# A decoder layer on one core: pacing of the routing pieces, batched one-hot comparisons and rearranged norms

## The chip, the cores and the metric

The kernel runs on one core of a Trainium2 chip. The metric is device time in microseconds (us), the median over executions. PE is the matmul engine, DVE the vector engine, ACT the scalar engine, POOL the GpSimd engine, SP the engine that mostly issues transfers. A change of under 0.3% (9.5 us here) can't be told from no change.

## The reference, cut to what matters

One layer over 512 tokens of width 2048, in fp32, batch 1, depth 1:

```python
n1 = rms_norm(h, norm1_gain)
q_lat, kv_lat, k_pe, q_swa, k_swa, v_swa = split(n1 @ w_in)         # 2048 x 2112
o_mla = mla_group(...)   # 8 heads, causal, latent q and kv, rotary key part
o_swa = swa_group(...)   # 16 heads, window 128, sinks, relative bias
h = h + concat(rms_norm(o_mla), rms_norm(o_swa)) @ w_out             # 2048 x 2048
xt = rms_norm(h, norm2_gain)
# PEER: 8 heads, two halves of 128 sub-keys each, 16384 experts
q = xt @ w_q;  s = einsum(q, sub_keys)                               # (512, 8, 2, 128)
s_half, i_half = top_k(s, 16)                                        # of 128
top_s, pos = top_k(all 256 sums of the two halves, 16)               # -> expert idx, g = softmax(top_s)
a = xt . expert_u[idx];  w = g * gelu(a)
h = h + sum over the 128 picked experts of w * expert_v[idx]
```

## The kernel before, in words

**Split matmuls.** An fp32 product is made of three matmuls. `split` (L115) writes the high part `hi` on ACT (L117) and the low part `lo` on DVE (L118), and PE multiplies hi·hi, hi·lo and lo·hi (L191 to L193; L897 to L899 in the expert stage). No weight reaches PE before DVE has written its `lo`; that instruction is kept in `mark[0]`. Weights arrive as raw tiles of 1 MB (two `wraw` and one `uraw`), and there are four pairs of part tiles.

**Stages.** In order of time, by the trace: the norm of x with its transposes (to 38 us), the w_in product (to 235), attention (to 470), output norms and w_out product (to 663), the second norm with its transposes (to 705), the w_q product (here `w_pq`, 709 to 883), the U stage (890 to 2074), the V stage (2074 to 3162).

**First norm (L239 to L251).** For each of four blocks of 128 tokens ACT squares and sums, POOL makes the factor `rs` of the root (`rsq`), DVE multiplies `xt` by `rs` and the gain in one instruction (L250), and PE transposes the product (L216).

**Second norm (L709 to L724).** DVE sums `squares` (L712), POOL makes `rs`, DVE writes `n2` in four quarters (L716) and PE transposes it. `n2` has one buffer, so block 1's quarters wait for block 0's transposes. For block 0 DVE also writes `xn0` (L721), the normed rows in their own layout, read by the gathered dot products only.

**U stage.** All 16384 experts are run densely for the last three token blocks (384 tokens), in 128 blocks of 128 experts. `u_block` (L889) has two halves of 24 matmuls. In each half `u_turn` (L876) traces the DVE transpose `uT` (L884) and the split of the half three ahead. The first 128 tokens are done otherwise: `gathered` (L971) fetches 128 rows of U and 128 batches of rows of V by indirect transfers of 1 MB on POOL's queue, with a dot product (L988) or a multiply-add (L991) on DVE for each: 256 gathered tiles in all.

**Fillers.** A `Filler` (L120) holds generators, and `run(budget)` takes pieces from them until their stated costs use the budget up. While it is `paced`, each piece is traced under `issue_after(mark[0])`: on DVE it stands behind the low part traced last. Otherwise the scheduler puts a piece by its priority and its estimate of when operands are ready. Routing (`route`, L756: top 16 by MAX8, FIND_INDEX8 and MATCH_REPLACE, then index arithmetic, all DVE) runs as such pieces, 3.6 per pair of weights in the w_q product and 2.8 per half block in the first U blocks (L1007), not paced. When all 16 routes are done, `dense_gates` (L913) starts as a filler: for each of 384 tokens it builds one-hot matrices of 128 by 128 (`oj` on POOL L921, `on` on DVE L923, `oi` on ACT L926), PE multiplies them into `gps` (L935), and ACT and DVE merge that into `stage` (L944, L945). Each full `stage` is stored to `gates_d` on ACT's queue (L947), 24 times. ACT's queue issues a part of each U load too (L872). The paced filler `gatherer` runs at 1.2 per half block in the U stage (L1035) and at 1.3 per step of 18 matmuls in the V stage (L1082), of which there are 256.

**V stage.** The dense weights `wg` (activations by gates, POOL L1055) are split and multiplied with V (L1065 to L1082), while the gathered tiles that are left run beside it.

## Time and profile before

| | |
|---|---|
| time, median of 3 runs | 3172.58 us (3164.42 to 3173.77) |
| profiled execution: its own time | 3167.54 us |
| its span | 3165.8 us |
| mean granted PE clock | 0.986 |
| PE busy | 3062.2 us, 97% |
| DVE busy | 2411.5 us, 76% |
| ACT, POOL busy | 1273.2 us, 1261.4 us |

A span is from the first to the last instruction; the time adds 1.7 us around it. Busy time is the sum of an engine's instruction times. The share is a mean over all stages; which engine is late in a stage is seen in the windows, which give the busy time of each engine in a stretch of the span, and in the list of PE's waits, which names the instruction that ended a wait.

### The profile page before, as it was taken

The page shows a single profiled execution, that of the slowest core. Times are in us where ns is not written, and L with a number is a line of the kernel's source. Part 1 is how long each engine was busy: PE and PEld are TensorE (multiplying, and loading weights), DVE is VectorE, ACT ScalarE, POOL GpSimd, SP SyncE. Part 2 cuts the span into 40 slices and gives each one's busy share as a digit, 9 for nine tenths or more (in the row PEclk, how much of TensorE's full clock was granted, in tenths as well). Part 3 has the DMA queues.
Part 4 walks back from the last instruction along what each step waited for, and adds up shares of the span by engine and source line. Part 5 has one row for each costly group of instructions (what it writes and reads, how often), then busy time and mean ns, then how long its engine had stood idle before and what let it go on. Part 6 is the DMA issues. An engine that isn't in the chain of part 4 may idle for free.

```text
span 3165.8 us, 43039 instructions
## 1 busy us (share of the span) xinstructions
PE 3062.2 (97%) x15418; PEld 2680.1 (85%) x15418; DVE 2411.5 (76%) x3774; ACT 1273.2 (40%) x2438; POOL 1261.4 (40%) x1324
## 2 busy tenths in 40 slices
PE   8999999989988998999999999999999999999999
PEld 6977767868778998999999998977888888888887
DVE  5425654246997897988999997878888878888784
ACT  5434443232234564655555553323333233232231
POOL 0115320001333765755556663244443334444430
PEclk9998999999999999999999999999999999999999
DMA  5422222244346899899899999989888878888873
GB/s 172 122 80 75 70 97 89 98 120 94 72 97 184 256 288 273 276 277 293 279 289 289 283 309 289 320 322 352 306 306 321 320 284 307 312 314 311 318 264 120
DMA packets 307064, 731.68 MB, mean 231 GB/s; under 512 B 24098, under 2 KB 106274, under 8 KB 269730
## 3 DMA queue, kind: packets, MB, share of 16 engines
q1 hardware_dynamic: 175394, 343.01, 34.6%
q0 software_dynamic: 45056, 293.63, 25.5%
q10 hardware_dynamic: 86400, 92.29, 10.6%
q8 instruction: 122, 2.00, 0.3%
q14 instruction: 92, 0.75, 0.1%
HBM read 666.97 MB, written 61.87 MB: 230 GB/s over the span
## 4 chain that ended last, share of the span: by engine, by line
PE 59%; DVE 12%; DMA 3%; issue 2%; ACTq 1%; ACT 1%; POOL 1%; SPq 0%; DVEq 0%; POOLq 0%
PE pa L899 8%; PE pa L897 8%; PE pa L898 8%; PE acc L191 8%; PE acc L193 8%; PE acc L192 8%; PE tp L191 4%; PE tp L193 3%; PE tp L192 3%; DVE wlo L118 2%; DVE uT L884 2%; DVE gt L988 2%; PE gps L935 1%; DMA wg<-acts_d 1%; ACTq L872 1%
## 5 line engine op out<-in xcount | busy, mean ns | idle before, releaser
L899 PE MATMUL pa<-xTd,wlo 128*128 128x384 f32 x1536 | 521.9, 340 | 12.7 <-DVE wlo L118 12.7
L118 DVE TENSOR_TENSOR wlo<-wraw,whi 128x1024 fp32r<-128x1024 f32 (+3 forms) x229 | 299.4, 1314 | 306.8 <-ACT whi L117 306.6
L897 PE MATMUL pa<-xTd,whi 128*128 128x384 f32 x1536 | 522.7, 340 | 4.1 <-ACT whi L117 4.0
L898 PE MATMUL pa<-xTd,whi 128*128 128x384 f32 x1536 | 521.1, 339 | 0.0
L921 POOL TENSOR_SCALAR oj<-iot,slT 128x128 fp32r<-128x128 f32 x384 | 391.7, 1028 | 295.6 <-PE gps L935 292.6
L117 ACT ACTIVATE whi<-wraw 128x1024 fp32r<-128x1024 f32 (+3 forms) x229 | 232.7, 1022 | 491.0 <-PE acc L193 251.1
L1055 POOL TENSOR_TENSOR wg<-wg,gg 128x384 f32<-128x384 f32 x128 | 231.6, 1828 | 265.3 <-DMA wg<-acts_d 229.9
L991 DVE SCALAR_TENSOR_TENSOR h<-gt,w,h 128x2048 f32<-128x2048 f32 x128 | 319.1, 2493 | 9.8 <-DMA gt<-in_peer_v_dram,eidx 9.8
L980 POOL DMA_INDIRECT gt<-in_peer_v_dram,eidx x128 | 197.1, 1540 | 302.0 <-DVE h L991 282.5
L191 PE MATMUL acc<-whi,wh 128*128 128x512 f32 x768 | 307.8, 401 | 5.5 <-ACT wh L117 5.5
L899 PEld LDWEIGHTS pa<-xTd,wlo 128*128 128x128 f32 x1536 | 292.7, 191 | 14.8 <-DVE wlo L118 14.8
L192 PE MATMUL acc<-wlo,wh 128*128 128x512 f32 x768 | 302.9, 394 | 2.1 <-DVE wlo L118 2.1
L193 PE MATMUL acc<-whi,wl 128*128 128x512 f32 x768 | 304.1, 396 | 0.2 <-DVE wl L118 0.2
L897 PEld LDWEIGHTS pa<-xTd,whi 128*128 128x128 f32 x1536 | 292.9, 191 | 5.7 <-ACT whi L117 5.4
L926 ACT ACTIVATE oi<-on,gT 128x128 fp32r<-128x128 bf16 x768 | 252.2, 390 | 108.8 <-issue 55.8
L988 DVE CUSTOM_DVE_ANT_0 gt<-gt,xn 128x2048 f32<-128x2048 f32 x128 | 293.2, 2291 | 2.9 <-DMA gt<-in_peer_u_dram,eidx 2.9
L898 PEld LDWEIGHTS pa<-xTd,whi 128*128 128x128 f32 x1536 | 292.6, 191 | 0.0
L118 DVE TENSOR_TENSOR wlo<-uT,whi 128x1024 fp32r<-128x1024 f32 x192 | 234.7, 1225 | 43.2 <-ACT whi L117 43.0
L117 ACT ACTIVATE whi<-uT 128x1024 fp32r<-128x1024 f32 x192 | 201.0, 1053 | 160.6 <-DVE uT L884 71.8
L191 PE MATMUL acc<-whi,xT 128*128 128x512 f32 (+2 forms) x624 | 239.7, 384 | 4.6 <-ACT xT L117 2.3
L192 PE MATMUL acc<-wlo,xT 128*128 128x512 f32 (+2 forms) x624 | 234.5, 376 | 4.2 <-DVE wlo L118 4.2
L193 PE MATMUL acc<-whi,xT 128*128 128x512 f32 (+2 forms) x624 | 235.4, 377 | 0.0
(305 smaller groups left out, 6710.8 us busy)
## 6 DMA issues: line engine op xcount, KB each, us to landing
wraw<-in_peer_v_dram SPq DMA_DIRECT2D x86, 1024.0 KB, 5.8
wraw<-in_peer_u_dram ACTq DMA_DIRECT2D x172, 256.0 KB, 7.5
wraw<-in_peer_u_dram SPq DMA_DIRECT2D x172, 256.0 KB, 6.2
uraw<-in_peer_v_dram SPq DMA_DIRECT2D x42, 1024.0 KB, 7.4
acts_d<-ga POOLq DMA_DIRECT2D x128, 192.0 KB, 6.9
gates_d<-stage ACTq DMA_DIRECT2D x24, 1024.0 KB, 13.9
gg<-gates_d SPq DMA_DIRECT2D x16, 1536.0 KB, 7.2
wg<-acts_d SPq DMA_DIRECT2D x128, 192.0 KB, 6.2
```

The source lines that it names most:

```text
L117: first[0] = nc.scalar.activation(hi, src, AF.Copy)
L118: mark[0] = nc.vector.tensor_tensor(lo, src, hi.bitcast(F32), op=ALU.subtract)
L191: nc.tensor.matmul(o, lhs(0, kk, t), w[0][:, k, :n], start=kk == 0, stop=False)
L192: nc.tensor.matmul(o, lhs(0, kk, t), w[1][:, k, :n], start=False, stop=False)
L193: nc.tensor.matmul(o, lhs(1, kk, t), w[0][:, k, :n], start=False, stop=kk == kc - 1)
L897: nc.tensor.matmul(pa[:, :TD], hi[:, k, :], xTd[0][:, kk, :], start=kk == 0, stop=False)
L898: nc.tensor.matmul(pa[:, :TD], hi[:, k, :], xTd[1][:, kk, :], start=False, stop=False)
L899: nc.tensor.matmul(pa[:, :TD], lo[:, k, :], xTd[0][:, kk, :], start=False, stop=kk == KC - 1)
L921: nc.gpsimd.tensor_scalar(oj, iot, slT[1][:, t:t + 1], None, op0=ALU.is_equal)
L926: nc.scalar.activation(oi[:, r, :], on, AF.Copy, scale=gT[r][:, t:t + 1].bitcast(F32))
L988: nc.vector.tensor_tensor_reduce(out=gt, in0=gt, in1=xn0, scale=1.0, scalar=0.0, op0=ALU.mult, op1=ALU.add, accum_out=a[:, s:s + 1])
L991: nc.vector.scalar_tensor_tensor(h[0], gt, w[:, s:s + 1], h[0], op0=ALU.mult, op1=ALU.add)
```

## The change

There are six edits. (1) The first norm's factor `rs` leaves L250: DVE multiplies by the gain alone, the factor is kept in a tile for each block, and the ACT copies that take the w_in product out of PSUM multiply by it. (2) `n2` gets three buffers, and `xn0` is traced after all four blocks of the second norm, behind the low part traced last. (3) The filler is paced from the w_q product until routing has ended. (4) Routing blocks take 1.4 per half instead of 2.8. (5) `on` is made for four tokens by one TENSOR_TENSOR of 128 by 512, 96 in all, with `slT[0]` in bf16. (6) The gatherer's budgets become 1.05 in the U stage and 1.5 in the V stage.

```diff
-        rs = rsq(ss, 1, D)
-        nc.vector.scalar_tensor_tensor(xt, xt, rs, g1, op0=ALU.mult, op1=ALU.mult)
+        rs1.append(rsq(ss, 1, D, name=f"rs1_{t}"))
+        nc.vector.tensor_tensor(xt, xt, g1, op=ALU.mult)
...
-        nc.scalar.activation(n, ps, AF.Copy)
+        nc.scalar.activation(n, ps, AF.Copy, scale=rs1[t])
...
-        n2 = p5n.tile([128, D], F32, name="n2")
+        n2 = p5n.tile([128, D], F32, name="n2", bufs=3)
...
-            nc.vector.scalar_tensor_tensor(xn0, h[0], rs, g2, op0=ALU.mult, op1=ALU.mult)
+            rs_first = rs
...
+    with tc.issue_after(mark[0].ins):
+        nc.vector.scalar_tensor_tensor(xn0, h[0], rs_first, g2, op0=ALU.mult, op1=ALU.mult)
...
+    filler.paced = True
     for c in range(4):
         gemm(stationary, KC, w_pq, c * 512, 512, ev_pq(c), budget=3.6, by_row=True, turn=c)
...
-        slT = [gb.tile([128, TD], F32, name=f"slT{r}") for r in range(2)]
+        slT = [gb.tile([128, TD], BF16 if r == 0 else F32, name=f"slT{r}") for r in range(2)]
...
-            on = gb.tile([128, NK], BF16, name="on", bufs=4)
-            nc.vector.tensor_scalar(on, iotb, slT[0][:, t:t + 1], None, op0=ALU.is_equal)
+            if t % 4 == 0:
+                ons[0] = gb.tile([128, 4, NK], BF16, name="on", bufs=2)
+                nc.vector.tensor_tensor(ons[0], iotb[:, None, :].to_broadcast([128, 4, NK]),
+                                        slT[0][:, t:t + 4, None].to_broadcast([128, 4, NK]), op=ALU.is_equal)
+            on = ons[0][:, t % 4, :]
...
-        u_block(e, 2.8)
+        u_block(e, 1.4)
...
+    filler.paced = False
     filler.add(dense_gates())
...
-        u_block(e, share, 1.2)
+        u_block(e, share, 1.05)
...
-                gatherer.run(1.3)
+                gatherer.run(1.5)
```

What the built program does with it, counted from both programs: routing ends with block 12 of the U stage before and with block 23 now; the dense gates lie over blocks 12 to 113 before and 23 to 117 now; of the 256 gathered tiles 122 are done in the U stage before and 96 now, so 134 and 160 are left to the V stage, where the last stands at step 237 of 256 before and 244 now. The counts of PE, ACT, POOL and SP instructions are the same; DVE has 288 fewer.

**DVE, the first U blocks.** `ulo` and `wlo` are low parts (L118), `uT` the transposes; MAX, MAX_INDEX, MATCH_REPLACE and what works on `ab`, `abf` and `oh` are routing. Before, these rows end a run of 24 routing rows that stands between one `uT` and the next low part:

```order
L786 TENSOR_TENSOR ab<-ab 128x32
L752 MATCH_REPLACE sc<-sv,sc 128x128
L787 CAST abf<-ab 128x32
L751 MAX_INDEX si<-sv,sc 128x8
L788 TENSOR_TENSOR ab<-ab 128x32
L793 TENSOR_TENSOR oh<-abf,iot 128x512
L789 TENSOR_TENSOR abf<-ab 128x32
L753 MAX sv<-sc 128x8
L793 TENSOR_TENSOR oh<-abf,iot 128x512
L118 TENSOR_TENSOR ulo<-uT,uhi 128x1024
L118 TENSOR_TENSOR wlo<-uT,whi 128x1024
L884 STREAM_TRANSPOSE uT<-uraw 128x4x8x32
```

In the change, at the same place of the stage (its lines are numbered three higher in `route`, four higher in `u_turn`):

```order
L118 TENSOR_TENSOR wlo<-uT,whi 128x1024
L753 MAX tv<-cand 128x8
L888 STREAM_TRANSPOSE uT<-uraw 128x4x8x32
L754 MAX_INDEX ti<-tv,cand 128x8
L888 STREAM_TRANSPOSE uT<-wraw 128x4x8x32
L755 MATCH_REPLACE cand<-tv,cand 128x65
L756 MAX tv<-cand 128x8
L757 MAX_INDEX ti<-tv,cand 128x8
L118 TENSOR_TENSOR wlo<-uT,whi 128x1024
L753 MAX tv<-cand 128x8
L118 TENSOR_TENSOR wlo<-uT,whi 128x1024
L754 MAX_INDEX ti<-tv,cand 128x8
```

The long run of routing rows between two low parts is now cut into runs of one to seven rows, each behind a low part.

**DVE, the second norm.** `ss` are the sums, `n_...` the quarters of `n2`, `xn_5857` is `xn0`, `h_...` the last merges of the w_out product. Before:

```order
L712 TENSOR_REDUCE ss<-squares 128x1
L721 SCALAR_TENSOR_TENSOR xn_5857<-h_4852,rs,g_4856 128x2048
L689 TENSOR_TENSOR h_4854<-acc,h_4854 128x512
L689 TENSOR_TENSOR h_4855<-acc,h_4855 128x512
L716 SCALAR_TENSOR_TENSOR n_5873<-h_4852,rs,g_4856 128x16x32 x2
L118 TENSOR_TENSOR wlo<-wraw,whi 128x1024
L716 SCALAR_TENSOR_TENSOR n_5873<-h_4852,rs,g_4856 128x16x32 x2
L712 TENSOR_REDUCE ss<-squares 128x1 x3
L118 TENSOR_TENSOR xT_5869<-tp,xT_5868 128x512 x4
```

In the change:

```order
L713 TENSOR_REDUCE ss<-squares 128x1
L690 TENSOR_TENSOR h_4854<-acc,h_4854 128x512
L713 TENSOR_REDUCE ss<-squares 128x1
L690 TENSOR_TENSOR h_4855<-acc,h_4855 128x512
L717 SCALAR_TENSOR_TENSOR n_5873<-h_4852,rs,g_4856 128x16x32 x4
L717 SCALAR_TENSOR_TENSOR n_5911<-h_4853,rs,g_4856 128x16x32
L118 TENSOR_TENSOR wlo<-wraw,whi 128x1024
L118 TENSOR_TENSOR xT_5869<-tp,xT_5868 128x512 x4
L717 SCALAR_TENSOR_TENSOR n_5911<-h_4853,rs,g_4856 128x16x32 x3
```

`xn_5857` has left its place behind the first sum, the second sum stands before the last merge, and a quarter of the second block stands ahead of the first transposed parts. `xn_5857` now stands behind the last transposed parts of the stage:

```order
L118 TENSOR_TENSOR xTd_5864<-tp,xTd_5863 128x4x128 x4
L717 SCALAR_TENSOR_TENSOR n_5989<-h_4855,rs,g_4856 128x16x32
L118 TENSOR_TENSOR xTd_5864<-tp,xTd_5863 128x4x128 x4
L727 SCALAR_TENSOR_TENSOR xn_5857<-h_4852,rs,g_4856 128x2048
L118 TENSOR_TENSOR ulo<-wraw,uhi 128x1024 x2
L118 TENSOR_TENSOR wlo<-uraw,whi 128x1024 x2
```

**ACT, the dense gates.** `gates_d<-stage` is the store of a full stage, `uraw` and `wraw` from `in_peer_u_dram` are the U loads on this queue. Before, around the first store:

```order
L944 ACTIVATE stage<-gps 128x2x16x8
L904 ACTIVATE ga<-pa 128x384
L117 ACTIVATE whi<-uT 128x1024
L947 DMA gates_d<-stage 128x16x128
L872 DMA uraw<-in_peer_u_dram 32x4x512 x2
L926 ACTIVATE oi<-on,gT_9174 128x128
```

In the change, the first store:

```order
L117 ACTIVATE uhi<-uT 128x1024
L117 ACTIVATE whi<-uT 128x1024
L954 DMA gates_d<-stage 128x16x128
L908 ACTIVATE ga<-pa 128x384
L951 ACTIVATE stage<-gps 128x2x16x8
L933 ACTIVATE oi<-on,gT_9933 128x128
L933 ACTIVATE oi<-on,gT_9934 128x128
L933 ACTIVATE oi<-on,gT_9933 128x128
L933 ACTIVATE oi<-on,gT_9934 128x128
L876 DMA wraw<-in_peer_u_dram 32x4x512 x2
```

Before, a U load follows the store directly; now six rows stand between the store and the next load.

## Rows read from the trace of the kernel before

**Rows 1.** The page, busy time, share of the span and instructions of each engine.

```profile
PE 3062.2 (97%) x15418; PEld 2680.1 (85%) x15418; DVE 2411.5 (76%) x3774; ACT 1273.2 (40%) x2438; POOL 1261.4 (40%) x1324
```

**Rows 2.** Waits of PE: us in total, times, the longest.

```profile
PE pa L899 <- DVE wlo L118: 12.7, 7, 7.6
PE gps L935 <- DVE stage L945: 12.7, 3, 10.3
PE tp L216 <- DVE xt L250: 11.1, 1, 11.1
PE tp L958 <- DVE ij L805: 8.9, 3, 4.1
PE tp L216 <- DVE ss L712: 6.8, 1, 6.8
```

**Rows 3.** Windows: length, busy (count) PE PEld DVE ACT POOL, PEclk, DMA share, GB/s.

```profile
650.00:700.00 50.00, 42.35 (x205) 34.22 (x205) 30.99 (x45) 15.60 (x28) 2.88 (x8) 0.93 0.47 132
800.00:850.00 50.00, 48.64 (x233) 39.62 (x231) 47.38 (x239) 13.27 (x19) 19.33 (x32) 1.00 0.34 78
850.00:900.00 50.00, 40.51 (x183) 33.10 (x184) 47.38 (x213) 10.62 (x15) 15.17 (x28) 0.93 0.40 90
900.00:950.00 50.00, 44.83 (x264) 43.72 (x263) 50.00 (x208) 22.67 (x28) 18.98 (x30) 0.97 0.42 97
950.00:1000.00 50.00, 41.59 (x209) 39.53 (x209) 41.83 (x124) 20.32 (x35) 21.72 (x27) 0.90 0.59 169
890.00:1000.00 110.00, 88.81 (x481) 85.16 (x480) 101.83 (x376) 44.35 (x66) 45.97 (x62) 0.92 0.48 125
1250.00:1300.00 50.00, 39.69 (x221) 39.31 (x220) 37.54 (x54) 24.11 (x59) 26.91 (x25) 0.90 0.86 265
2100.00:2150.00 50.00, 47.89 (x205) 37.94 (x204) 48.27 (x45) 15.65 (x20) 24.89 (x14) 1.00 0.94 362
```

**Rows 4.** Windows of line L897 alone (16 per block): length, PE, PEld, clock, DMA.

```profile
890.40:993.50 103.10, 45.71 (x129) 25.76 (x128) 0.92 0.46 120
993.50:1096.60 103.10, 63.87 (x191) 35.75 (x190) 1.00 0.82 232
```

**Rows 5.** Timeline of DVE, 884 to 900: start, us, instruction.

```profile
886.41 0.24 DVE L753 MAX8 sv<-sc 128x8 f32<-128x128 f32 x1
...
897.28 2.40 DVE L118 TENSOR_TENSOR wlo<-uT,whi 128x1024 fp32r<-128x1024 f32 x2
```

**Rows 6.** Groups of DVE instructions, 890 to 1000: busy us, mean ns.

```profile
L118 DVE TENSOR_TENSOR wlo<-uT,whi 128x1024 fp32r<-128x1024 f32 x15 | 17.9, 1223 | 0.0
L884 DVE STREAM_TRANSPOSE uT<-wraw 128x1024 f32<-128x1024 f32 x13 | 15.5, 1214 | 0.0
L793 DVE TENSOR_TENSOR oh<-abf,iot 128x512 f32<-128x512 f32 x12 | 11.2, 932 | 0.0
```

**Rows 7.** Timeline of DVE, 663 to 674.

```profile
662.85 2.35 DVE L721 SCALAR_TENSOR_TENSOR xn<-h,rs,g 128x2048 f32<-128x2048 f32 x1 [0.94 <-POOL rs L113]
...
672.07 0.69 DVE L118 TENSOR_TENSOR xT<-tp,xT 128x512 fp32r<-128x512 f32 x1 [1.71 <-ACT xT L117]
```

**Rows 8.** Timeline of DVE, 0 to 24.

```profile
8.71 2.35 DVE L250 SCALAR_TENSOR_TENSOR xt<-xt,rs,g 128x2048 f32<-128x2048 f32 x1 [5.08 <-POOL rs L113]
```

**Rows 9.** Line L923, DVE: ns min/median/max, first and last start.

```profile
L923 DVE TENSOR_SCALAR on<-iotb,slT x384: 201/247/607, 993.7 to 1924.0; 128x128 bf16<-128x128 bf16 x192
```

**Rows 10.** Timeline of ACT, 1245 to 1270.

```profile
1246.62 0.39 ACTq L947 DMA_DIRECT2D gates_d<-stage  x1
...
1252.70 10.96 ACTq L872 DMA_DIRECT2D uraw<-in_peer_u_dram  x2
1263.70 0.69 ACT L926 ACTIVATE oi<-on,gT 128x128 fp32r<-128x128 bf16 x2 [15.18 <-issue]
```

**Rows 11.** Windows: the long middle of the expert stages.

```profile
1050.00:2050.00 1000.00, 977.25 (x5680) 973.13 (x5679) 894.12 (x1223) 536.94 (x1246) 586.08 (x595) 0.99 0.96 289
2150.00:3100.00 950.00, 949.87 (x4071) 764.06 (x4070) 786.05 (x636) 290.13 (x337) 389.10 (x233) 1.00 0.83 307
```

More of the change, by code (lines that the diff above doesn't have):

```diff
@@ L105, in gain_rows, with rsq @@
         return t
-    def rsq(ss, n, width, post=1.0):
-        r = small.tile([128, n], F32, name="rs", tag=f"rs{n}")
+    def rsq(ss, n, width, post=1.0, name=None):
+        r = small.tile([128, n], F32, name=name, bufs=1) if name else small.tile([128, n], F32, name="rs", tag=f"rs{n}")
         with tc.high_priority(offset=150):
@@ L238, in block_kernel @@
     p0 = pool("p0", bufs=2, stack=st0)
+    rs1 = []
     for t in range(NT):
@@ L323, in ev_kv @@
         w = KVR + ROPE
-        nc.scalar.activation(n[:, :w], ps[:, :w], AF.Copy)
+        nc.scalar.activation(n[:, :w], ps[:, :w], AF.Copy, scale=rs1[t])
         nc.scalar.activation(sq[:, :KVR], n[:, :KVR], AF.Square, accum_out=ss)
@@ L340, in ev_ks @@
         n = p1w.tile([128, QR], F32, name="latn", bufs=4)
-        nc.scalar.activation(n[:, :2 * HD], ps[:, :2 * HD], AF.Copy)
-        nc.scalar.activation(vsw[:, t, :], ps[:, 2 * HD:4 * HD], AF.Copy)
+        nc.scalar.activation(n[:, :2 * HD], ps[:, :2 * HD], AF.Copy, scale=rs1[t])
+        nc.scalar.activation(vsw[:, t, :], ps[:, 2 * HD:4 * HD], AF.Copy, scale=rs1[t])
         k3 = n[:, :2 * HD].rearrange("p (g d) -> p g d", g=2)
@@ L359, in f @@
             qn = p1w.tile([128, QR], F32, name="latn", bufs=4)
-            nc.scalar.activation(qn, ps, AF.Copy)
+            nc.scalar.activation(qn, ps, AF.Copy, scale=rs1[t])
             q3 = qn.rearrange("p (h d) -> p h d", h=8)
@@ L913, in dense_gates @@
     def dense_gates():
-        slT = [gb.tile([128, TD], F32, name=f"slT{r}") for r in range(2)]
+        slT = [gb.tile([128, TD], BF16 if r == 0 else F32, name=f"slT{r}") for r in range(2)]
         gT = [gb.tile([128, TD], F32R, name=f"gT{r}") for r in range(2)]
-        hot, banks, stages = {}, {}, {}
+        hot, banks, stages, ons = {}, {}, {}, {}
         LAG = 7
```

## The prediction

> **What bounds the kernel now.** I read the page first, then PE's waits, then the windows of the stages where they fall, and only then the timelines. The page has PE busy for 97% of the span [rows 1], so what can be won is PE's idle time, what a lowered clock costs after it, and nothing else: the matmuls are the same before and after. PE's waits say where [rows 2]: on low parts in the U stage (12.7 us in seven waits, one of 7.6), on the merge of the dense gates (12.7, one of 10.3), on the first norm (11.1), on the index sums of routing (8.9) and on the second norm (6.8). Four of these five name DVE instructions that the change moves. The windows [rows 3] show how they bunch: the four from 800 to 1000 have PE busy for 48.64, 40.51, 44.83 and 41.59 of 50, which is 24.4 us of idle time. The granted clock there is 1.00, 0.93, 0.97 and 0.90, a mean of stretches at 2.4 GHz and, after idle times, at 1.2; a shortfall of the clock can cost at most 50 us times that shortfall, 10.0 together. DVE is at 47.38, 47.38 and 50.00 of 50 in the first three of them: there DVE is the bound. Beside it, line L897, 16 times per block, is there 129 times in 103.1 us and then 191 times in the same length [rows 4]: eight blocks at 12.9 us against twelve at 8.6. By this the first eight blocks lose 34 us, of which the idle time and the clock explain nearly all.
>
> The reason is a matter of order. From 886.41 to 897.28 DVE runs routing [rows 5] and only then the two low parts for which PE waits 7.6 us. DVE had the work of a later need ahead of that of a nearer one.
>
> **The change, part by part.**
>
> Routing in the first U blocks (paced, 1.4 for 2.8). DVE's work in a block now: from 890 to 1000 it is busy for 101.83 [rows 3]. Low parts are 1.22 us each, transposes 1.21 [rows 6], and a block has two of each: 4.9. In 110 us, at 12.9 each for the most part, are nine blocks or so, 44 us of such work, which leaves 58 us of routing, 6.4 per block at 2.8 per half. At 1.4 it is half, 3.2. DVE then has 4.9 + 3.2 = 8.1 us per block against PE's 8.6: it fits, by 6%. No piece stands ahead of a low part already traced, so a low part is delayed by one run of pieces (up to seven rows of about 0.28 us, some 2 us) instead of 10.9. Routing lasts until block 23 instead of 12, at no cost to PE while DVE fits. What is late next are the transposes of the index sums: they are ordered among PE's matmuls behind DVE's last reduces, and I leave 3 of their 8.9 us; another 1 to 2 go to the start of the stage. Of 34.4 us (24.4 and 10.0) I take 30 as gone. Bounds: 34 at best, and 13 if DVE stays a little too slow for 23 blocks (below). The same pacing in the w_q product orders the same work at the same budget; its loss in [rows 3] is only 1.4 us, counted above.
>
> Second norm. `xn0`, 2.35 us [rows 7], stands ahead of the last merges and quarters for which PE waits 6.8 us; now it stands behind the stage, and with three buffers the next block's first quarter comes earlier. The wait shrinks by 2.35 and by some of the 0.9 us that DVE waits for POOL ahead of it. The window 650 to 700 has a clock of 0.93 [rows 3], worth up to 3.5 us, part of which goes with it. I take 4; bounds 0 (another operand is as late) and 10 (all of it). `xn0` at its new place is read first by the gathered tiles hundreds of microseconds later.
>
> First norm. DVE waits 5.08 us for the factor `rs` in block 0 [rows 8], and PE's first transpose waits behind that. Without the factor DVE waits for the transfer of `xt` and the gain. Bounds 0 and 5.1, and I take the half, 2.5, since weights must land too before the first product. The multiplication returns inside ACT's copies, which exist anyway: nothing added.
>
> Batched comparisons. 384 instructions at 0.247 [rows 9] are 95 us of DVE. The 96 new ones aren't in this trace. Nearest are two-operand instructions of 512 elements: 0.69 for a low part `xT` [rows 7], 0.93 for `oh` [rows 6], the latter with the same broadcast shape. Below lies 0.25, were 512 elements no dearer than 128. The range is 24 to 89 us, I take 0.69: 66 us, 29 less. All of it lies beside PE at full work: from 1050 to 2050 PE is at 977 of 1000 and DVE at 894 [rows 11]. So it is slack, counted at nothing, unless DVE were the later one at the stalls.
>
> Against this edit speaks a rule of the Trainium skill ("VectorE: DVE Perf Modes", section "The perf-mode tier table"): a comparison with one scalar may run at four elements a cycle in bf16, one with two tensors at two at most, and only with 16-bit operands of step 1, which the broadcast hasn't. By its fp32 formula, (N+151)/0.96 ns, 512 elements are an estimated 0.69 us, 66 us in all; at two a cycle it would be about 0.42, 41 us. The old row's minimum of 201 ns [rows 9] agrees with the fast mode and a large fixed part, so batching gains by the fixed part and loses the mode. Either price is hidden, and the sum above is the same by both.
>
> Dense gates. These begin 11 blocks later and are a little denser (94 blocks for 101). The costly event there isn't DVE's. At 1252.70 two U loads on ACT's queue take 10.96 us to issue, six microseconds after the store of a gate stage, ACT stands for 15.18 [rows 10], and the merge that PE waits for comes 10.3 late [rows 2]; the window loses 10.3 idle and up to 5.0 by the clock of 0.90 [rows 3]. PE's idle time from 1050 to 2050 is 22.7 us in all [rows 11], with the clock's 0.01 below full up to 10 more. Each of the 24 stores and the loads are still there. Their distances change at random: at the first store a load stood directly behind it, and now six rows lie between. I take 5 us less; bounds -26 and +18, the latter being one more stall of that size with its clock.
>
> V stage. 26 gathered tiles move there from the U stage, 27 MB and about 2.3 us of DVE each. From 2150 to 3100 PE is busy for 949.87 of 950, DVE for 786 and the transfers run at 307 GB/s [rows 11]. Adding 26 in some 1040 us makes DVE 84 to 88% busy and 333 GB/s. The window 2100 to 2150 reached 362 with DVE at 48.27 of 50 [rows 3], so both fit. The last tile stands at step 244 of 256, so no tail. I take 0; bounds 0 and +89 (below).
>
> Sum: 30 + 4 + 2.5 + 5 = 41.5. The profiled execution took 3167.5, which gives 3126; it lies 5 below the median of 3172.6, from which it would be 3131. I say 3128.
>
> **The rivals.**
>
> DVE stays the bound in the routing blocks. It is 8.1 of 8.6 by my division, and a fifth more routing per block than I assume (3.8) makes it 8.7, with waits on POOL's products inside the pieces still to come. At 9.2 per block, 23 blocks lose 14 us beyond the forecast; with clock, 17: 3145. For it: DVE was at 50.00 of 50 from 900 to 950. Against: halving is a plain division of a measured load.
>
> The stores' stalls vanish. With DVE lighter and loads further from stores, 26 of the 33 us of the dense stage go instead of 5: 3107. For it: the distance at the first store. Against: the two queues still share what made the load slow, and with 24 stores some will meet a load.
>
> The V stage becomes the bound, the slower side. If transfers can't go beyond the stage's 307 GB/s, the 27 MB cost 27/0.307 = 89 us, and the sum is 3128 + 89 = 3217. It decides from 51 us upward (the gain of 41.5 and the 9.5 that can be told), which 346 MB in the stage need below some 317 GB/s. A milder form is that the whole stage goes like the window 2100 to 2150, PE at 47.89 of 50: 1088 us become 1136, and with 3176 it is no change. For it: PE had waits in just that window, where transfers were busiest. Against: those waits are at the stage's beginning, while later windows have PE full at 307.
>
> The change doesn't do what it says: the tie adds waits of its own and routing delays PE in 23 blocks as it did in 12. Then only the norms' 6.5 count, and 3166 is within the bound. Against: the new order shows low parts at the head of each portion.
>
> **How the numbers follow.** The forecast, 3112 to 3141, has 0.60; DVE still the bound, 3141 to 3160, 0.15; the stalls gone, 3095 to 3112, 0.10; the V stage 0.09, of which 0.05 is slower and 0.04 no change; without effect 0.06, mostly no change, 0.01 slower. A measurement tells 0.3%, 9.5 us, from no change, so faster is below 3163: 0.60 + 0.15 + 0.10 = 0.85; no change 0.04 + 0.05 = 0.09; slower 0.06. The range 3100 to 3158 leaves out the last two rivals and the far ends of the others, about 0.19.
>
> **What would show it.** Right: from 890 on, line L897's blocks come every 8.3 to 8.8 us from the first one, PE has no wait for a low part above 2 us there, and the clock stays at 1.00 from 800 to 1000; DVE is near 47 of 50 until about 1100. PE's first wait ends near 8 to 9 us instead of 11.1, the second norm's wait is 3 to 4 us instead of 6.8, `on` takes 0.65 to 0.75 us, and the V stage has PE full at some 333 GB/s. Wrong: blocks of 9 us and more up to 1100, idle time of PE behind gathered transfers or low parts after 2150, or a store's stall of 10 us more than now.

## The result: 3123.8 us, and two misses of opposite sign

The changed kernel takes 3123.77 us (median of 4 runs, 3121.87 to 3131.22) against 3170.64 for the kernel before (4 runs). The ratio is 0.9856, with a 95% interval of 0.9837 to 0.9874: 47 us less by the medians, 1.4% by the ratio. The forecast was 3128, with a range of 3100 to 3158. The profiled execution is the slowest of the four, 3131.2 us with a span of 3129.5, so the traces account for 36 us of the difference.

The windows say where. First the kernel before, in windows that join those of [rows 3] (length; busy time and count of PE, PEld, DVE, ACT, POOL; granted clock; share of the transfer engines; GB/s):

```profile
750.00:1050.00 300.00, 275.57 (x1419) 247.20 (x1418) 274.04 (x1065) 107.82 (x175) 107.30 (x168) 0.97 0.46 113
1050.00:1900.00 850.00, 833.92 (x4870) 831.91 (x4869) 770.91 (x1104) 487.36 (x1168) 534.35 (x549) 0.99 0.95 287
...
2074.00:2150.00 76.00, 68.34 (x275) 53.43 (x276) 60.95 (x56) 24.20 (x35) 36.79 (x23) 0.96 0.90 343
2150.00:3090.00 940.00, 939.87 (x4029) 755.99 (x4028) 779.46 (x628) 286.95 (x334) 389.10 (x233) 1.00 0.83 307
```

The changed kernel, by the same view. It comes to its V stage at 2012, 61 us earlier:

```profile
650.00:700.00 50.00, 45.69 (x227) 37.23 (x226) 30.64 (x45) 16.85 (x30) 2.88 (x8) 0.97 0.46 137
750.00:1050.00 300.00, 299.56 (x1610) 275.61 (x1609) 278.44 (x964) 101.64 (x130) 80.10 (x135) 1.00 0.50 119
1050.00:1900.00 850.00, 850.00 (x4971) 849.63 (x4970) 762.03 (x902) 515.92 (x1254) 496.13 (x575) 1.00 0.93 274
...
2000.00:2050.00 50.00, 44.20 (x196) 36.32 (x195) 36.53 (x35) 17.82 (x26) 20.35 (x15) 0.97 0.81 301
2050.00:2100.00 50.00, 40.75 (x159) 31.79 (x158) 36.49 (x35) 10.90 (x13) 21.97 (x12) 0.90 0.85 319
2100.00:2150.00 50.00, 45.79 (x188) 35.94 (x188) 44.14 (x42) 12.82 (x14) 23.06 (x16) 0.97 0.90 331
2150.00:3090.00 940.00, 933.91 (x3989) 749.58 (x3988) 799.20 (x651) 283.09 (x330) 435.07 (x242) 1.00 0.88 323
```

From 750 to 1050 PE's idle time went from 24.4 us to 0.4, and the clock from 0.97 to 1.00. From 1050 to 1900 it went from 16.1 us to none, and the clock from 0.99 to 1.00. From the V stage's start to 2150 it grew from 7.7 us to 19.3, with a clock down to 0.90, and after that from 0.1 us to 6.1. A ledger that also counts what half clock costs takes each matmul's distance to the next one and the median distance of its shape in the kernel before, and sums by stage what the first has over the second (us lost):

| stage | before | after | difference | forecast |
|---|---|---|---|---|
| first norm to w_out product (0 to 650) | 84.7 | 84.8 | 0 | -2.5 |
| second norm (650 to 750) | 18.1 | 13.0 | -5 | -4 |
| w_q product and first U blocks (750 to 1050) | 36.5 | 2.2 | -34 | -30 |
| rest of the U stage | 35.8 | 13.9 | -22 | -5 |
| V stage | 18.9 | 44.1 | +25 | 0 |
| sum | 194 | 158 | -36 | -41.5 |

PE's waits in the changed kernel, to be set against [rows 2]:

```profile
PE acc L192 <- DVE wlo L118: 17.6, 10, 6.6
PE tp L216 <- DVE xt L251: 11.2, 1, 11.2
PE acc L192 <- DVE ulo L118: 7.9, 4, 3.5
...
PE tp L216 <- DVE n L717: 3.5, 1, 3.5
...
PE pa L903 <- DVE wlo L118: 0.8, 2, 0.4
```

The low parts of the U stage, 12.7 us before, are down to 0.8 and the gates' merge is gone from the list. On top stand low parts at L192 of `acc`, 25.5 us in 14 waits; all but one wait of 2.2 us, at 22.9 in the w_in product, are in the V stage. The blocks of the U stage come at an even pace, one in 8.3 us, from the third one on (the first two take 12.3 and 10.8); line L901 is what L897 was in [rows 4], and the eight blocks of 12.9 us have become twelve of 8.6:

```profile
887.50:990.60 103.10, 64.39 (x192) 35.85 (x192) 1.00 0.60 145
```

### The profile page after: what moved, and what is told of

The parts are those of the page before. It is cut to its first block, busy times and chain, and to the rows that moved or that the text cites. A ratio compares the mean times of both kernels' runs of the same rounds, so it can differ in the third digit from the quotient of the medians.

```text
span 3129.5 us, 42706 instructions
## 1 busy us (share of the span) xinstructions
PE 3055.9 (98%) x15418; PEld 2676.6 (86%) x15418; DVE 2408.1 (77%) x3486; ACT 1274.6 (41%) x2438; POOL 1237.2 (40%) x1324
## 4 chain that ended last, share of the span: by engine, by line
PE 77%; DMA 8%; DVE 7%; issue 3%; POOL 3%; ACT 1%; SPq 0%; ACTq 0%; POOLq 0%; DVEq 0%
PE pa L903 11%; PE pa L901 11%; PE pa L902 11%; PE acc L192 10%; PE acc L191 10%; PE acc L193 10%; DMA wg<-acts_d 4%; PE tp L192 2%; PE tp L191 2%; PE tp L193 2%; DVE h L998 2%; PE gps L942 1%; DVE wlo L118 1%; POOL wg L1063 1%; DMA wraw<-in_peer_v_dram 1%
## 5 line engine op out<-in xcount | busy, mean ns | idle before, releaser
L901 PE MATMUL pa<-xTd,whi 128*128 128x384 f32 x1536 | 518.5, 338 | 1.1 <-ACT whi L117 1.1
L903 PE MATMUL pa<-xTd,wlo 128*128 128x384 f32 x1536 | 515.2, 338 | 0.9 <-DVE wlo L118 0.8
L118 DVE TENSOR_TENSOR wlo<-wraw,whi 128x1024 fp32r<-128x1024 f32 (+3 forms) x229 | 294.3, 1290 | 287.8 <-ACT whi L117 287.3
L925 POOL TENSOR_SCALAR oj<-iot,slT 128x128 fp32r<-128x128 f32 x384 | 320.3, 844 | 299.9 <-PE gps L942 295.8
L1063 POOL TENSOR_TENSOR wg<-wg,gg 128x384 f32<-128x384 f32 x128 | 248.3, 1951 | 232.8 <-DMA wg<-acts_d 209.3
L192 PE MATMUL acc<-wlo,wh 128*128 128x512 f32 x768 | 306.9, 400 | 15.5 <-DVE wlo L118 15.4
L995 DVE CUSTOM_DVE_ANT_0 gt<-gt,xn 128x2048 f32<-128x2048 f32 x128 | 301.0, 2351 | 25.1 <-DMA gt<-in_peer_u_dram,eidx 25.1
L987 POOL DMA_INDIRECT gt<-in_peer_v_dram,eidx x128 | 211.1, 1649 | 248.4 <-DVE h L998 218.6
L901 PEld LDWEIGHTS pa<-xTd,whi 128*128 128x128 f32 x1536 | 288.3, 188 | 2.1 <-ACT whi L117 2.1
L902 PEld LDWEIGHTS pa<-xTd,whi 128*128 128x128 f32 x1536 | 288.4, 188 | 0.0
L118 DVE TENSOR_TENSOR wlo<-uT,whi 128x1024 fp32r<-128x1024 f32 x192 | 237.8, 1249 | 40.4 <-ACT whi L117 39.3
L192 PE MATMUL acc<-wlo,xT 128*128 128x512 f32 (+2 forms) x624 | 235.0, 377 | 2.3 <-DVE wlo L118 2.2
```

Of the source, the lines that this page charges most:

```text
L118: mark[0] = nc.vector.tensor_tensor(lo, src, hi.bitcast(F32), op=ALU.subtract)
L192: nc.tensor.matmul(o, lhs(0, kk, t), w[1][:, k, :n], start=False, stop=False)
L901: nc.tensor.matmul(pa[:, :TD], hi[:, k, :], xTd[0][:, kk, :], start=kk == 0, stop=False)
L902: nc.tensor.matmul(pa[:, :TD], hi[:, k, :], xTd[1][:, kk, :], start=False, stop=False)
L903: nc.tensor.matmul(pa[:, :TD], lo[:, k, :], xTd[0][:, kk, :], start=False, stop=kk == KC - 1)
L925: nc.gpsimd.tensor_scalar(oj, iot, slT[1][:, t:t + 1], None, op0=ALU.is_equal)
```

## The experiments

Each was timed beside the kernel before. "The changed kernel" is 3123.8 us throughout, from the runs above; it wasn't timed again beside them, so a small difference from it is read by the ratios to the kernel before (0.9837 to 0.9874 for the changed kernel).

**The tie or the portion: each alone.** First the tie away:

```diff
-    filler.paced = True
     for c in range(4):
```

> The changed kernel without the tie of the routing pieces behind the low parts, still 1.4 per half block. Theory A (the order is what mattered: runs of pieces ahead of the low parts): PE waits on low parts from 800 to 1050 come back, 10 to 25 us, time 3135 to 3150. Theory B (the halved portion is what mattered): within 6 us of the changed kernel, 3118 to 3130.

Measured: 3161.67 us (3154.62 to 3166.74), ratio to before 0.9968 (0.9955 to 0.9981). Its windows:

```profile
850.00:900.00 50.00, 42.37 (x196) 34.98 (x194) 47.32 (x213) 12.59 (x18) 15.14 (x28) 0.91 0.41 90
900.00:950.00 50.00, 43.49 (x256) 42.55 (x255) 50.00 (x207) 20.70 (x26) 19.30 (x30) 0.98 0.41 100
950.00:1000.00 50.00, 42.83 (x221) 40.63 (x220) 41.80 (x119) 21.84 (x38) 23.15 (x27) 0.92 0.61 177
```

This is the loss of the kernel before, window by window [rows 3], although the portion is 1.4. DVE shows why, start and duration first:

```profile
880.91 2.35 DVE L887 STREAM_TRANSPOSE uT<-wraw 128x1024 f32<-128x1024 f32 x2
...
894.07 2.40 DVE L118 TENSOR_TENSOR wlo<-uT,whi 128x1024 fp32r<-128x1024 f32 x2
```

Between the transposes and the next low parts still lie 10.8 us, and they are routing: without the tie the scheduler puts ready pieces there whatever budget they were traced under. Routing ends at 970 here, as in the kernel before (974), where the changed kernel needs until 1074. Theory A holds, with a time 12 us above its range, since the routing loss comes back whole; the portion alone takes nothing of it.

Then the tie kept, with the old portion:

```diff
-        u_block(e, 1.4)
+        u_block(e, 2.8)
```

> The changed kernel with 2.8 per half block instead of 1.4, still tied. Theory A (order alone): within 8 us of the changed kernel. Theory B (amount: 4.9 us of low parts and transposes and 6.4 of routing per block are more than PE's 8.6): DVE is the bound in the first dozen blocks, which take 11 to 12 us each, 25 to 40 us more than the changed kernel, 3149 to 3164.

Measured: 3178.56 us (3174.56 to 3191.62), ratio to before 1.0028 (1.0015 to 1.0041): 55 us slower than the changed kernel, and slower than before.

```profile
900.00:950.00 50.00, 46.24 (x262) 44.57 (x261) 48.00 (x162) 13.04 (x17) 14.15 (x22) 1.00 0.46 114
950.00:1000.00 50.00, 43.70 (x217) 41.77 (x218) 49.52 (x188) 17.42 (x21) 14.21 (x28) 0.90 0.46 116
1000.00:1050.00 50.00, 35.66 (x165) 32.24 (x164) 42.61 (x98) 27.90 (x68) 32.84 (x35) 0.83 0.63 180
```

PE idles for 24.4 us in these three windows, with a clock down to 0.83. DVE is nearly full in the first two (48.00 and 49.52 of 50): there the amount doesn't fit, as theory B has it. The third window, with 14.3 of the 24.4 us, is another matter, since DVE has room in it (42.61). On DVE:

```profile
1019.73 1.22 DVE L808 TENSOR_REDUCE ij<-oh 128x64 f32<-128x1024 f32 x1 [2.37 <-POOL oh L802]
```

One of the last routing pieces waits 2.4 us there for a product on POOL, with a low part behind it for which PE waits 5.4, and the start of the dense gates costs another 4.1 (PE waits for ACT's `oi`). So a tied piece that waits for another engine holds up the low part behind it, beside the amount. Theory B holds in part, and the time is 15 us above its range. By the ledger some 41 of the 54 us between the two traces lie from 750 to 1050, and the rest is spread (6 in the V stage, with one wait of 10.7 at 2124). The two runs together show that the gain of 34 us needs both edits.

**The tie and the portion without the other edits**, in the kernel before:

```diff
+    filler.paced = True
     for c in range(4):
...
-        u_block(e, 2.8)
+        u_block(e, 1.4)
...
+    filler.paced = False
     filler.add(dense_gates())
```

> The kernel before with the tie and 1.4 per half block alone: old norms, single one-hot comparisons, gatherer at 1.2 and 1.3 (by its counts some 2 tiles are left behind the last V step, up to 6 us). Theory A (parts add up: routing is worth 34 us, the dense gates keep their stalls): PE is full from 750 to 1050, long issues on ACT's queue sum to 40 us or more, time 3138 to 3150. Theory B (a later start of the dense gates alone takes the stalls away): 3120 to 3135.

Measured: 3155.58 us (3148.68 to 3159.55), ratio 0.9947 (0.9928 to 0.9967).

```profile
750.00:1050.00 300.00, 299.58 (x1612) 275.17 (x1611) 278.53 (x975) 99.42 (x127) 79.55 (x137) 1.00 0.49 118
1100.00:1900.00 800.00, 778.41 (x4530) 773.99 (x4529) 729.22 (x1075) 475.99 (x1172) 535.02 (x546) 0.99 0.95 284
```

The first row has the routing gain in full. The second has the stalls of the dense gates, 21.6 us of idle time in 800, where the kernel before has 16.1 in 850: a later start alone doesn't take them away, and long issues on ACT's queue (over 1.5 us, see below) sum to 64 us. DVE ends 10.6 us after PE's last matmul (3.7 in the changed kernel), which is the tail of gathered tiles that a V pace of 1.3 leaves, and the V stage's start costs more than before here too. Theory A, with a time a little above its range for these two costs.

**What took the dense gates' stalls away: lighter gathering?**

```diff
-        u_block(e, share, 1.05)
+        u_block(e, share, 1.2)
...
-                gatherer.run(1.5)
+                gatherer.run(1.35)
```

> The changed kernel with the gatherer at 1.2 per half block in the U stage (1.05) and 1.35 per step in the V stage (1.5): 13 tiles go back to the U stage. Theory A (the fuller V stage costs: gathered tiles land late at its start and stand in front of low parts on DVE): PE's idle time from the V stage's start on falls from 24 us by 8 to 15, the dense gates stay without long waits, and the time is 6 to 14 us below the changed kernel's 3124. Theory B (the lighter gathering in the U stage is what took the dense gates' stalls away): waits of PE on the gates' merge come back, 10 to 25 us, and the time is 3125 to 3140.

Measured: 3145.25 us (3140.73 to 3149.3), ratio 0.9916 (0.9903 to 0.9929), 21 slower than the changed kernel. From 1100 to 1900 PE idles for 11.2 us again (none in the changed kernel). On ACT, in the stretch of the longest wait:

```profile
1507.38 0.39 ACTq L954 DMA_DIRECT2D gates_d<-stage  x1
1511.17 9.57 ACTq L876 DMA_DIRECT2D wraw<-in_peer_u_dram  x2
1520.78 1.06 ACT L117 ACTIVATE whi<-uT 128x1024 fp32r<-128x1024 f32 x1 [12.42 <-issue]
```

It is the picture of [rows 10]: two U loads 3.8 us behind a gate store take 9.6 us to issue, and ACT stands for 12.4. The issues of over 1.5 us on ACT's queue between 1050 and 2000 sum to 58 us before, 11 in the changed kernel and 49 here. Transfers from 1100 to 1900 run at 288 GB/s on the mean of four windows, against 280 in the changed kernel and 286 before. Theory B holds, with a time 5 us above its range, and PE's waits are now for high parts from ACT (12.0 us in five), not for the gates' merge. Theory A fails: the V stage's first windows lose as much at 1.35 (18.7 us of idle time from 2000 to 2150) as at 1.5.

**Is it the queue?** The same paces, with the gate stores on SP:

```diff
-                nc.scalar.dma_start(
+                nc.sync.dma_start(
                     bass.AP(tensor=gates_d.tensor, ...
```

> The kernel with the gatherer at 1.2 and 1.35 (3145), and the 24 stores of gate stages issued by SP instead of ACT. Theory A (a U load on ACT's queue issues slowly because it follows a store of 2048 pieces on the same queue while gathered tiles load the transfer engines): long issues on ACT (49 us in that run) fall below 10 us, PE's idle time from 1100 to 2000 falls from 14 to under 6, time 3122 to 3132. Theory B (the transfer engines are short of room, whoever issues): the loss stays within 5 us, 3140 to 3150, or SP's loads behind the stores come late and it is longer.

Measured: 3132.26 us (3127.41 to 3139.62), ratio 0.9876 (0.9854 to 0.9898), 13 less than with the stores on ACT.

```profile
1100.00:1900.00 800.00, 799.07 (x4660) 798.41 (x4659) 740.01 (x829) 491.67 (x1213) 435.58 (x560) 1.00 0.95 294
```

Long issues on ACT fall from 49 us to 1.7 and PE idles for 0.9 us from 1100 to 1900; on SP they sum to 24, which PE doesn't feel. The transfers run at 294 GB/s there, more than with the stores on ACT, so it is the place behind the store on the same issuing queue that costs. Theory A.

**Is it also the batch?** The old comparison, with four buffers (shown) and with eight (`bufs=8`); `slT[0]` is fp32 again in both:

```diff
-            if t % 4 == 0:
-                ons[0] = gb.tile([128, 4, NK], BF16, name="on", bufs=2)
...
+            on = gb.tile([128, NK], BF16, name="on", bufs=4)
+            nc.vector.tensor_scalar(on, iotb, slT[0][:, t:t + 1], None, op0=ALU.is_equal)
```

> The changed kernel with the one-hot comparison again by one TENSOR_SCALAR per token and four buffers of 128. Theory A (the stalls of the dense gates were passed on from ACT to DVE through the four buffers, and eight tokens in two batches give DVE room): stalls come back, waits of PE on the merge of 8 to 20 us, time 3133 to 3150. Theory B (the batch is only DVE slack, and the stalls went because the loads come later behind the stores or the gathering is lighter): no change, within 5 us of the changed kernel.

> The changed kernel with the one-hot comparison by one TENSOR_SCALAR per token and eight buffers (four in the run before, 3138.5). Theory A (the four buffers passed ACT's stalls on to DVE): PE's idle time from 1100 to 1900 falls from 11 us to 4 or less, time 3122 to 3131. Theory B (it is DVE's time, 0.25 per token against 0.68 per four, or where instructions stand): still 3135 to 3143.

Measured: with four buffers 3138.54 us (3136.95 to 3141.83), ratio 0.9895 (0.988 to 0.9909); with eight 3129.70 us (3119.78 to 3132.08), ratio 0.9866 (0.9844 to 0.9888). With four:

```profile
1100.00:1900.00 800.00, 788.98 (x4612) 786.23 (x4611) 722.24 (x1078) 489.31 (x1198) 526.43 (x544) 0.99 0.92 275
```

With eight:

```profile
1100.00:1900.00 800.00, 800.00 (x4669) 800.00 (x4669) 725.71 (x1091) 495.00 (x1220) 435.44 (x550) 1.00 0.95 279
```

PE's idle time in this stretch is 11.0 us with four buffers and none with eight, as in the changed kernel. DVE's time for the comparison isn't the cause, since a single one takes 0.25 us in both. DVE's waits for ACT to free a buffer of `on`, first in the kernel before, then with four buffers:

```profile
DVE on L923 <- ACT oi L926: 28.9, 14, 11.8
DVE on L927 <- ACT oi L930: 21.9, 15, 5.0
```

With eight buffers, and in the changed kernel, this wait isn't there at all. So what counts is how far DVE may run ahead of ACT before a comparison without a free buffer blocks the low parts behind it; the batch brought room for eight tokens in place of four. With neither the batch nor the lighter gathering (the kernel with the tie and the portion alone) PE idles for 21.6 us here, with one of them for 11.2 or 11.0, with both for none. Long issues fell as well (22 us with four buffers, 4 with eight), so this run doesn't tell how much of the loss was passed on and how much didn't arise. Whether eight single comparisons are equal to the batch, within 6 us, stays open: the ranges overlap.

**The first norm.** The gain in quarters:

```diff
-                nc.sync.dma_start(g1, rows(norm1_gain, 0, D))
+                for c0 in range(0, D, 512):
+                    nc.sync.dma_start(g1[:, c0:c0 + 512], rows(norm1_gain, c0, 512))
...
-        nc.vector.tensor_tensor(xt, xt, g1, op=ALU.mult)
+        for c0 in range(0, D, 512):
+            nc.vector.tensor_tensor(xt[:, c0:c0 + 512], xt[:, c0:c0 + 512], g1[:, c0:c0 + 512], op=ALU.mult)
```

> The changed kernel with the first norm's gain loaded and multiplied in four quarters of 512 columns. In the changed kernel DVE waits for the gain's transfer where it waited for the factor before. Theory A (the whole gain's landing is what is late): PE's first transposes start at 7 to 9 us instead of 11.2. Whether the time follows: if the first weights' low part, at 22.9, is the end of that stage anyway, PE's later waits grow by as much and the time is within 3 us of 3124; if not, 2 to 4 us less.

Measured: 3129.08 us (3125.22 to 3136.95), ratio 0.986 (0.9837 to 0.9883). PE's timeline:

```profile
8.96 3.81 PE L216 MATMUL tp<-ident,xt 128*128 128x128 f32 x16 [8.96 <-POOL rs L111]
...
24.70 1.63 PE L191 MATMUL acc<-whi,xT 128*128 128x512 f32 x3
```

The transposes do start at 8.96 instead of 11.2. But the first product, which in the changed kernel starts at 20, waits for a low part and goes on at 22.9, starts at 24.7 here. Nothing is won: by the ratios (0.986 and 0.9856) the two can't be told apart, and by the ledger this trace loses 3.6 us more up to 650. The start of PE's first work isn't the end of this stage.

**The V stage's start.** No gathered tile in its first 16 steps:

```diff
-                gatherer.run(1.5)
+                if g:
+                    gatherer.run(1.6)
```

> The changed kernel with no gathered tile traced in the V stage's first 16 steps and 1.6 per step after them (1.5). Theory A (at the V stage's start gathered tiles land late, their dot products stand in front of low parts on DVE, and PE waits): PE's idle time from the stage's start (2012) to 2150 falls from 20 us to 8 or less, time 3105 to 3115. Theory B (the start is short of transfers of weights and gates, gathered tiles or not): idle time stays at 15 or more, time 3120 to 3130; the fuller rest of the stage may add some.

Measured: 3107.11 us (3104.23 to 3113.69), ratio 0.9799 (0.9778 to 0.9819), 17 us below the changed kernel, with ranges that don't meet.

```profile
2000.00:2050.00 50.00, 48.04 (x214) 40.18 (x213) 32.96 (x33) 19.33 (x28) 17.28 (x13) 0.97 0.85 313
2050.00:2100.00 50.00, 50.00 (x216) 40.26 (x215) 38.19 (x34) 16.16 (x20) 24.76 (x14) 1.00 0.67 236
2100.00:2150.00 50.00, 48.94 (x209) 38.79 (x208) 40.50 (x43) 13.40 (x16) 15.32 (x11) 1.00 0.86 323
```

Idle time there is 3.0 us in place of 19.3. Theory A: gathered tiles at that place cost the time, not weights or gates.

**The two remedies together**: stores on SP, 1.2 in the U stage, and a free start.

```diff
-        u_block(e, share, 1.05)
+        u_block(e, share, 1.2)
...
-                gatherer.run(1.5)
+                if g:
+                    gatherer.run(1.45)
```

> The changed kernel with no gathered tile in the V stage's first 16 steps, the 24 gate stores on SP's queue, and the gatherer at 1.2 in the U stage and 1.45 after the first 16 steps. Theory A (the two losses are separate: the stores cost through ACT's queue, the V stage's start through late gathered tiles): PE's idle time from 1100 to 1900 is under 3 us though 13 tiles more are gathered there, under 6 from 2000 to 2150, and the later V stage loses less than the 7 us at 1.6; time 3098 to 3106, below the 3107 of the kernel with the free start alone. Theory B (the fuller U stage pushes stalls elsewhere, SP's loads among them): 3108 to 3120.

Measured: 3132.03 us (3121.22 to 3137.38), ratio 0.9876 (0.9855 to 0.9896): not better but 25 worse than the free start alone. Both remedies do their part (1.0 us idle from 1100 to 1900, 5.2 from 2000 to 2150), but after 2150 PE loses 20.7 us, most in three waits of 5.7 to 6.9. Before the first of them, on POOL:

```profile
2327.79 9.28 POOL L1063 TENSOR_TENSOR wg<-wg,gg 128x384 f32<-128x384 f32 x3 [7.63 <-DMA wg<-acts_d]
2337.22 0.98 POOL L987 DMA_INDIRECT gt<-in_peer_v_dram,eidx  x1 [0.15 <-issue]
```

and on DVE:

```profile
2345.66 2.35 DVE L998 SCALAR_TENSOR_TENSOR h<-gt,w,h 128x2048 f32<-128x2048 f32 x1 [9.75 <-DMA gt<-in_peer_v_dram,eidx]
2347.93 1.22 DVE L118 TENSOR_TENSOR wlo<-wraw,whi 128x1024 fp32r<-128x1024 f32 x1
```

POOL waits 7.6 us for a load of activations, takes 9.3 for three products, and only then issues the transfers of gathered tiles; DVE waits 9.8 for the tile, with a low part behind it for which PE waits 6.9. Theory B, with a time 12 us above its range, and a slower V pace is no safeguard.

**The loads of activations on ACT**, in both of these kernels:

```diff
-            nc.sync.dma_start(wgs[e], acts_d[e])
+            nc.scalar.dma_start(wgs[e], acts_d[e])
```

> The kernel with the free V start and 1.6 (3107.1), the loads of activations for `wg` issued by ACT instead of SP. Theory A (the chain is: SP issues these loads late behind V loads that wait for their buffers, POOL's product stands in front of the gathered transfer, its axpy in front of a low part): POOL's waits for `wg`'s load, 196 us there, fall under 100, DVE's waits for gathered tiles, 23 us, under 10, PE loses under 3 us after 2150 instead of 7; time 3100 to 3106. Theory B (the gathered transfers are slow by themselves at 325 GB/s): the waits for tiles stay at 15 to 30 us, time 3105 to 3112. ACT's own waits for buffers may also delay high parts: then 3110 to 3125.

> The same edit in the kernel with stores on SP, 1.2 and 1.45 (3132.0), which lost 20 us after 2150 in three waits of 6 to 7 us. Theory A: these waits go, PE loses under 4 us after 2150; time 3100 to 3112. Theory B: two or three waits of this size stay, time 3120 to 3135.

Measured: in the kernel with the free start 3106.52 us (3100.91 to 3112.57), ratio 0.9806 (0.9791 to 0.9821), no change from 3107.1; in the other 3122.82 (3122.17 to 3125.91), ratio 0.9854 (0.9839 to 0.9869), 9 less by the medians, but the intervals of the two ratios overlap. In the first one's trace, an execution of 3101.5 us, PE is full after 2150:

```profile
2150.00:3090.00 940.00, 939.63 (x4026) 755.81 (x4025) 824.82 (x666) 282.18 (x325) 440.01 (x248) 1.00 0.89 330
```

But POOL's waits for these loads only fell from 196 us to 163, DVE's waits for gathered tiles didn't fall (27.3 us, 23.0 without the edit), and the five times spread over 12 us: by its waits and its time this is theory B, and only PE's loss after 2150 goes as theory A has it. In the second kernel 5.7 us of the 20.7 are left, the longest wait is 4.2, and the time lies in theory B's range. So the late load may be one link of the chain, which these runs don't show beyond their noise, and it isn't all of it. The best kernel is the changed one with the free V start, 3107 us, with the loads on either queue.

## Why the prediction was right, and where it wasn't

**Routing.** Right, with its reason: 34 us measured, 30 taken of a loss of 34.4. DVE is at 278.4 of 300 from 750 to 1050 and PE full; the division (8.1 of 8.6 us per block) held, and the two runs with one edit each show that neither the order nor the portion does it alone. I left 4 us for the index sums and the stage's start, and it was 2. The rival that DVE stays the bound is out at 1.4, and is a part of what happens at 2.8.

**Second norm.** Right: the wait is 3.5 us instead of 6.8, 5 us with the clock, 4 taken. The kernel with the tie and the portion alone has the old order there and waits 6.8 us, so the gain belongs to this edit.

**First norm.** Wrong. I took 2.5 us and it was nothing. DVE in the changed kernel:

```profile
8.74 2.29 DVE L251 TENSOR_TENSOR xt<-xt,g 128x2048 f32<-128x2048 f32 x1 [5.11 <-DMA g<-in_norm_gain_dram]
```

The multiplication starts at 8.74 instead of 8.71 [rows 8]: the gain lands when the factor used to be ready. The lower bound named this case, and I should have asked when the next operand lands before taking half. The quarters show that an earlier start of the first transposes is worth nothing by itself there; they also split DVE's work in all four blocks, so what the start alone would give isn't shown.

**Batched comparisons.** The size was right:

```profile
L928 DVE TENSOR_TENSOR on<-iotb,slT x96: 644/676/858, 1090.4 to 1879.8; 128x512 bf16<-128x512 bf16 x96
```

0.68 us against 0.69 taken. The Trainium skill ("VectorE: DVE Perf Modes", section "What auto-detection actually checks") gives a two-source op two elements a cycle only if every tensor is 16-bit with step 1 or -1. The trace agrees with the slow rate for this broadcast operand (0.68 us, where the prediction's estimate at two a cycle was 0.42), though no run changes the operand alone. What I got wrong is that it was "slack, counted at nothing": not its time but its buffers had a price.

**Dense gates.** The mechanism was right, loads slow to issue behind a store on ACT's queue, and the size wrong: 22 us, 5 taken. I put the change down to chance in the distances. The runs show two causes that I had as separate edits at nothing, the lighter gathering in the U stage and the room that the batch gives DVE: undoing either brings 11 us of idle time back. The rival "The stores' stalls vanish" came true as to the stalls, but its two reasons aren't shown: a lighter DVE isn't needed (eight single comparisons, as dear as before, have no stalls either), and the distance of loads from stores was tried only by moving the stores to SP. Its 3107 us didn't come because of the V stage.

**V stage.** Wrong step: "I take 0", since DVE at 88% and 333 GB/s "both fit". The rates do fit; after 2150 the transfers run at 323 GB/s. The loss is in the order, as it was in the routing blocks, and one of the signs of being wrong that I had named is there, idle time behind low parts after 2150 (6.1 us). On POOL, then DVE, in the changed kernel's longest wait:

```profile
2065.02 10.24 POOL L1063 TENSOR_TENSOR wg<-wg,gg 128x384 f32<-128x384 f32 x4 [1.39 <-DMA wg<-acts_d]
2075.41 1.78 POOL L987 DMA_INDIRECT gt<-in_peer_u_dram,eidx  x1 [0.15 <-issue]
```

```profile
2074.03 2.31 DVE L118 TENSOR_TENSOR wlo<-wraw,whi 128x1024 fp32r<-128x1024 f32 x1
2083.96 2.29 DVE L995 CUSTOM_DVE_ANT_0 gt<-gt,xn 128x2048 f32<-128x2048 f32 x1 [7.62 <-DMA gt<-in_peer_u_dram,eidx]
...
2086.18 1.22 DVE L118 TENSOR_TENSOR wlo<-wraw,whi 128x1024 fp32r<-128x1024 f32 x1
```

The products of `wg` stand in front of the transfer's issue, the transfer lands 8.5 us later, DVE waits 7.6 for it, and the low part behind it (2086.18) ends PE's wait of 6.6. Through waits like this the V stage lost 25 us more than before, and with no gathered tile at its start PE idles for 16 less from 2000 to 2150. In size the 25 us are half of the milder form that I gave this rival (48 us), by another mechanism than transfers at their limit. That the 26 moved tiles brought it is not shown: with the tie and the portion alone, where none is moved, PE idles for 17.3 us from 2000 to 2150 too, and with 13 of them moved back for 18.7.

So the time came out within 5 us because the two large misses, 17 us better in the dense gates and 25 worse in the V stage, have opposite signs, which is luck; the sum of the terms was 41.5, the traces have 36. The profiled run of the changed kernel lies 7 us above its median, and that of before 3 below its own.

What stays open: why the kernel before lost only 19 us in its V stage, while the eight other kernels here that gather at the stage's start lost 29 to 50, by the same ledger. The one with its own paces (1.2 and 1.3) and the tie lost 29, so the pace alone isn't it. Why single waits of 6 us come at other places with other paces, as in the kernel with both remedies, wasn't settled either.

## What to carry to other kernels

An engine that has time enough by its rates can still be late by its order: what stands in front of the instruction that the busiest engine waits for must be counted as a run, not as a share. Pinning a filler behind that instruction and cutting its portion to what fits belong together; either alone gave nothing of the routing gain here, and the tie alone made the kernel slower. Where work is moved to another stage, look at that stage's first 100 us by itself, on each in-order queue through which the moved work passes.

## What the runs showed of the hardware

Two U loads on the same queue, 4 to 6 us behind a store of 2048 pieces of 512 bytes, took up to 9.6 and 11.0 us to issue, where most take 0.8. Issues of over 1.5 us fell from 49 us to 11 when fewer gathered tiles were fetched beside them (all traffic at 280 GB/s instead of 288). The rate alone doesn't set it: they sum to 22 us at 275 GB/s with the four buffers, and to 1.7 on ACT at 294 with the stores on SP.

POOL's product of 128 by 384 and DVE's low part of 128 by 1024 are slower beside each other. In the V stage of the changed kernel 176 low parts ran beside no such product, none longer than 1.23 us; of the 77 that ran beside one, 34 took over 2 us and the longest 4.1 (at 2074.03 above, 2.31). The product has a median of 1.5 us; the 11 that ran beside no DVE instruction took 1.4 at most, the others up to 5.3, and in the two groups shown that stood before PE's long waits they took 2.6 and 3.1 on the mean. So a part of the run in front of the gathered transfers is this slowing, which the prediction's rates don't have; no run here takes one of the two away from the other.
